# A two-layer encoder on one core: 17 of 44 pairs of W_up's row tiles with seven block products for eight

## The chip, the cores and the metric

The kernel runs on one core of a Trainium2 chip. The metric is device time in microseconds (us) of one execution; lower is better. The inputs lie in device memory when the time begins.

## What is computed

Two layers over 512 positions of 1024 channels, all in float32. The part around the change is the feed-forward block; the rest of a layer is a Fourier group and a windowed attention with 8 heads, joined by W_o.

```python
def reference(x, ...):                      # x: (1, 512, 1024)
    for l in range(2):
        p = rmsnorm(x, norm1[l]) @ w_in[l]
        u, q, k, v = split(p)               # 512 Fourier columns, 8 heads, 2 key and value heads
        y_f = fourier_mix(u, w_fourier[l], b_fourier[l])     # Re(FFT2(u)) @ w_f + b_f
        y_a = windowed_gqa(rope(rmsnorm(q)), rope(rmsnorm(k)), v, sink[l])
        x = x + concat(rmsnorm(y_f), rmsnorm(y_a)) @ w_o[l]
        h = rmsnorm(x, norm2[l])
        up = dwconv_centred(h @ w_up[l], conv_w[l], conv_b[l])   # 3 taps over positions
        gate, val = split(up)               # 2816 columns each
        x = x + (silu(gate) * val) @ w_down[l]
    return x
```

## The kernel before

**Data.** x stays in SBUF, transposed: eight tiles x[k] of 128 channels x 512 positions. A matrix product is made of matmuls with a 128x128 block of weights and up to 512 columns of data. To keep float32's precision, both operands are split into a high and a low part, and mm3 (L114) issues three matmuls into one PSUM bank: high x high (L120), low x high (L121), high x low (L122). Weights are split on the way: wload (L127) loads 512 KB into one of three wraw buffers on SP's queue, wsplit (L132) lets ACT copy the high part of a 512-column chunk into one of five whi buffers and DVE subtract it, for one of five wlo buffers (L140, recorded at L93 with every other tensor_tensor; ACT's instructions are all at L90).

**Names.** A tile's name is its buffer's tag with a number: tF and tA are general temporaries of 512 columns (six each), sq the temporary of squares (two), m4, slab, act and pT larger ones; rb is a row of reciprocal norms copied from PSUM, and nr, computed on POOL at L211, what it is made from. PSUM has eight banks: mm (three), sc (two), tp (two), av (one); the feed-forward block uses six of them in turn (FFN_BANKS). Numbers in the quoted rows tell tiles of one tag apart.

**Order.** The kernel is written for a tile framework: the program gives the operations, and a scheduler with a model of the engines decides in which order each engine's instructions stand; buffers and banks are handed out in the order of the program, and a tile waits until its buffer's last one is done with. issue_after holds an instruction back behind another. Every engine then runs its own list strictly in that order.

**Attention and W_o.** attention(p) (written from L513) treats two heads: for each block of 128 queries PE makes scores (L529), DVE masks them, ACT takes exponentials with their sum, POOL divides (L538), PE transposes (L541), ACT copies the result out of PSUM as pT, PE multiplies with the values (L548). The order in the program is attention(3), attention(0), the Fourier group's output (L634 to L661, tile yf), attention(1), attention(2), W_o. Its first half (L683) needs the Fourier group alone (ys), so that its 96 matmuls can be spread among the steps of attention(1) and (2); mm3's after= and the list steps do that. Its second half (L690) needs the attention. It updates x, and norm_tile makes h2, the split, scaled input of the feed-forward block, with the sum of squares for rb2, the row of reciprocal norms that is multiplied in behind W_up.

**Feed-forward block** (L705 to L761). The 22 tiles of gate columns and the 22 of value columns are paired: pair fi is made of tiles fi and fi + 22. Each tile takes 8 blocks x 3 matmuls of 512 columns, then DVE multiplies by rb2 out of PSUM, ACT and DVE make the three-tap convolution (an activation and two scalar_tensor_tensor at L96), ACT applies silu, the two tiles are multiplied (DVE in layer 0, POOL in layer 1) and split into gu. After 11 pairs W_down's eight tiles take these as input (HALVES). presplit splits layer 1's W_qkv, W_in, W_fourier and W_o during layer 0 and stores the two parts in DRAM, from where layer 1 fetches them; it goes one step ahead at a time, with next(ahead).

## Time and profile before

| | |
|---|---|
| time, median of 3 runs | 1057.46 us (1056.27 to 1057.54) |
| the profiled execution | 1056.14 us, span 1054.3 us |
| granted TensorE clock | 0.999 |
| matmuls | 5107, busy 1038.2 us |
| HBM read, written | 116.02 MB, 23.07 MB |
| W_up | 88 loads of 512.0 KB |

The profile is of one execution. Its engines are PE (matmuls), PEld (loading of weights into PE, beside PE's work), DVE (vector), ACT (scalar), POOL and SP (here a DMA queue). A busy time is the sum over an engine's instructions; what bounds a stage is seen in the stage's own rows, and in what ended the idle time before an instruction ("<-").

### The profile page before, as it was taken

What the parts mean: (1) busy time and instruction counts of PE and PEld (TensorE: products, weight loads), DVE (VectorE), ACT (ScalarE), POOL (GpSimd) and SP (SyncE); (2) the same over time, 40 slices, a digit from 0 to 9 for tenths busy, and PEclk for the clock granted to TensorE, in tenths of its full rate; (3) what the DMA queues carried; (4) which work ended last, traced back from release to release, by engine and by line L of the source; (5) the groups of instructions that cost most, each with busy time, mean ns of one, the idle gap of its engine ahead of it and who ended that gap; (6) DMA issues with size and microseconds to landing.
All of it is one profiled execution on the core that took longest, in us unless ns stands there. A gap on an engine that the chain in (4) does not pass through costs nothing.

```text
span 1054.3 us, 14425 instructions
## 1 busy us (share of the span) xinstructions
PE 1038.2 (98%) x5107; PEld 873.2 (83%) x5107; DVE 726.8 (69%) x1384; ACT 507.9 (48%) x939; POOL 90.8 (9%) x164
## 2 busy tenths in 40 slices
PE   8998999999999999999999999999999999999998
PEld 8986778888888888888899887888888888888887
DVE  8878768697767777777519775478877336878632
ACT  5339755455444445455423785246554224454421
POOL 0004410000000000000000152001101000101100
PEclk9999999999999999999999999999999999999999
DMA  7232152332269833239856313333332333332241
GB/s 273 83 115 87 58 193 81 100 100 96 78 226 353 324 100 101 89 114 322 280 181 221 113 62 99 122 100 94 101 101 74 96 115 100 98 101 82 82 150 48
DMA packets 60475, 140.03 MB, mean 133 GB/s; under 512 B 6642, under 2 KB 22258, under 8 KB 60404
## 3 DMA queue, kind: packets, MB, share of 16 engines
q1 hardware_dynamic: 60404, 139.12, 40.5%
q8 instruction: 40, 0.66, 0.3%
q14 instruction: 31, 0.25, 0.1%
HBM read 116.02 MB, written 23.07 MB: 132 GB/s over the span
## 4 chain that ended last, share of the span: by engine, by line
PE 93%; DVE 2%; DMA 2%; ACT 1%; issue 1%; POOL 0%; SPq 0%; ACTq 0%; DVEq 0%; POOLq 0%
PE ps L122 28%; PE ps L120 28%; PE ps L121 28%; PE ps L118 3%; PE ps L548 2%; PE ps L541 2%; PE ps L529 1%; DMA wraw<-in_w_qkv_dram 1%; PE ps L234 1%; PE ps L227 1%; ACT tA L90 0%; DMA x<-in_xT_dram 0%; DVE tA L533 0%; ACT act L90 0%; PE ps L500 0%
## 5 line engine op out<-in xcount | busy, mean ns | idle before, releaser
L90 ACT ACTIVATE whi<-wraw 128x512 fp32r<-128x512 f32 (+1 forms) x296 | 182.0, 616 | 290.8 <-PE ps L122 278.4
L120 PE MATMUL ps<-act,whi 128*128 128x512 f32 x768 | 298.9, 390 | 0.0
L121 PE MATMUL ps<-act,wlo 128*128 128x512 f32 x768 | 298.3, 389 | 0.0
L122 PE MATMUL ps<-act,whi 128*128 128x512 f32 x768 | 298.2, 389 | 0.0
L93 DVE TENSOR_TENSOR wlo<-wraw,whi 128x512 fp32r<-128x512 f32 (+1 forms) x304 | 219.7, 726 | 103.4 <-ACT whi L90 102.0
L122 PEld LDWEIGHTS ps<-act,whi 128*128 128x128 f32 x768 | 144.2, 188 | 30.1
L120 PEld LDWEIGHTS ps<-act,whi 128*128 128x128 f32 x768 | 144.2, 188 | 29.7
L121 PEld LDWEIGHTS ps<-act,wlo 128*128 128x128 f32 x768 | 144.2, 188 | 29.7
L96 DVE SCALAR_TENSOR_TENSOR tF<-tF,pb,tF 128x511 f32<-128x511 f32 x176 | 133.5, 763 | 11.1 <-ACT tF L90 8.7
L93 DVE TENSOR_TENSOR tF<-ps,rb 128x512 f32<-128x512 f32 x104 | 71.2, 689 | 77.9 <-PE ps L122 64.7
L120 PE MATMUL ps<-slab,whi 128*128 128x512 f32 (+2 forms) x212 | 82.2, 388 | 0.0
L122 PE MATMUL ps<-slab,whi 128*128 128x512 f32 (+2 forms) x212 | 79.9, 380 | 0.4 <-DVE slab L93 0.3
L121 PE MATMUL ps<-slab,wlo 128*128 128x512 f32 (+2 forms) x212 | 80.0, 378 | 0.0
L90 ACT ACTIVATE tF<-tF,pb 128x512 f32<-128x512 f32 x88 | 71.7, 816 | 11.3 <-DVE tF L93 4.6
L93 DVE TENSOR_TENSOR x<-x,ps 128x512 f32<-128x512 f32 (+1 forms) x49 | 32.9, 674 | 36.5 <-PE ps L122 36.3
L93 POOL TENSOR_TENSOR tF<-tF,tF 128x512 f32<-128x512 f32 x22 | 30.2, 1371 | 256.1 <-DVE tF L96 224.1
L120 PE MATMUL ps<-pT,whi 128*128 128x512 f32 (+1 forms) x132 | 50.5, 383 | 0.0
L121 PE MATMUL ps<-pT,wlo 128*128 128x512 f32 (+1 forms) x132 | 50.5, 383 | 0.0
L122 PE MATMUL ps<-pT,whi 128*128 128x512 f32 (+1 forms) x132 | 50.5, 383 | 0.0
L538 POOL TENSOR_SCALAR tA<-tA,den 128x256 f32<-128x256 f32 (+1 forms) x64 | 37.4, 590 | 145.1 <-DVE den L537 144.6
L533 DVE CUSTOM_DVE_ANT_0 tA<-ps,pb,nsink 128x256 f32<-128x256 f32 (+1 forms) x64 | 37.8, 603 | 14.5 <-PE ps L529 9.7
L122 PEld LDWEIGHTS ps<-slab,whi 128*128 128x128 f32 x212 | 39.7, 188 | 8.3 <-DVE slab L93 0.9
(178 smaller groups left out, 1485.0 us busy)
## 6 DMA issues: line engine op xcount, KB each, us to landing
wraw<-in_w_up_dram SPq DMA_DIRECT2D x88, 512.0 KB, 3.5
wraw<-in_w_down_dram SPq DMA_DIRECT2D x32, 512.0 KB, 3.7
kept<-tA SPq DMA_DIRECT2D x56, 256.0 KB, 5.7
whi<-kept SPq DMA_DIRECT2D x28, 256.0 KB, 3.0
wlo<-kept SPq DMA_DIRECT2D x28, 256.0 KB, 3.0
kept<-tA SPq DMA_DIRECT2D x32, 192.0 KB, 4.4
wraw<-in_w_down_dram SPq DMA_DIRECT2D x32, 192.0 KB, 2.4
wraw<-in_w_o_dram SPq DMA_DIRECT2D x8, 512.0 KB, 3.7
```

The lines of the kernel that those rows point to most:

```text
L90: return nc.scalar.activation(out, in_, func, **kw)
L93: return (eng or nc.vector).tensor_tensor(out, a, b, op=op)
L96: return nc.vector.scalar_tensor_tensor(out=out, in0=a, scalar=s, in1=b, op0=op0, op1=op1)
L118: nc.tensor.matmul(out, a[0], b[0], start=start, stop=stop, **kw)
L120: nc.tensor.matmul(out, a[0], b[0], start=start, stop=False, **kw)
L121: nc.tensor.matmul(out, a[1], b[0], start=False, stop=False, **kw)
L122: nc.tensor.matmul(out, a[0], b[1], start=False, stop=stop, **kw)
L227: nc.tensor.matmul(pt[:, 2 * b:2 * b + 2], acc[:, b * P:(b + 1) * P], ones2, start=True, stop=True)
L533: nc.vector.tensor_tensor_reduce(out=pr[:, :n], in0=sc[:, :n], in1=mask[:, m0:m0 + n], scale=qs_scale[p][:, i, e:e + 1], scalar=nsink[:, l ...
L538: nc.gpsimd.tensor_scalar(pr[:, :n], pr[:, :n], den[:, i:i + 1], 1.0, op0=ALU.mult, op1=ALU.mult)
L541: tr = nc.tensor.transpose(pp[:, j * P:(j + 1) * P], pr[:, j * P:(j + 1) * P], ident)
L548: pv = nc.tensor.matmul(py[64 * e:64 * e + 64, i0 * P:(i1 + 1) * P], vp[:, j, 64 * g:64 * g + 64], pT[:, half, e, b0:b0 + 2 * (i1 - i0) + ...
```

## The change

A pair's two tiles and the eight tiles of h make a product of 2 x 2 blocks: the weights' blocks are a11, a12 (tile fi, first and last four k), a21, a22 (tile fi + 22), and h's are first and last four k, positions 0 to 255 and 256 to 511. Block by block this takes eight block products. In 17 of the 44 pairs (layer 0: fi = 2, 5, 8, 11, 14, 17, 20; layer 1: fi = 3, 5, ..., 21) up_seven now takes seven, of sums and differences of blocks, each of 4 k x 3 matmuls of 256 columns. DVE makes the weights' sums (s1 to s4) and all seven low parts; the products are accumulated in PSUM and, between the banks, by ACT's copies and DVE's additions. The sums of h's blocks are made once for a layer (sums_of_h), in the buffers m4, room and others that are free by then.

The other pairs go through up_eight. For one tile of the pair in layer 0 and for both in layer 1 it makes the low part another way (wsplit_add): ACT writes the negated high part to wlo, and a DMA on POOL's queue reads the same weights from DRAM a second time and accumulates them on it (256 KB each, 78 in all).

Besides: three groups of 8, 7 and 7 pairs for two of 11; silu's product on DVE in both layers; the square's temporary from sq to tF everywhere, in attention too; presplit with one matrix part at a time, in a buffer praw of its own, and its ACT copy held behind the pair's last ACT step (pace).

```diff
-HALVES = [(0, 11), (11, 11)]
+GROUPS = [(0, 8), (8, 7), (15, 7)]
+SEVEN = [range(2, FT, 3), range(3, FT, 2)]
...
-             "tA": (512, 6), "tF": (512, 6), "sq": (512, 2)}
+             "tA": (512, 6), "tF": (512, 6), "praw": (512, 2)}
...
+    def wsplit_add(raw, src):
+
+        hi, lo = [wp.tile([P, 512], F32R, tag=z, name=nm(z), bufs=5) for z in ("whi", "wlo")]
+        act(hi, raw)
+        act(lo, f(hi), scale=-1.0)
+        nc.gpsimd.dma_start(lo, src, accum_op=ALU.add)
+        return hi, lo
...
-    def add_square(acc, src, first, tag="sq"):
+    def add_square(acc, src, first, tag="tF"):
...
+    def sums_of_h(l, h2):
+
+        room = rooms()
+        out = []
+        for k in range(4):
+            b = [temp(512, "tF") for _ in range(2)]
+            for i in range(2):
+                act(b[i], x[k + 4 * i], scale=g2[:, l, k + 4 * i:k + 4 * i + 1])
+            t13, t24 = temp(512, "tF"), temp(512, "tF")
+            tt(t13[:, LO], b[0][:, HI], b[0][:, LO], ALU.subtract)
+            tt(t13[:, HI], b[1][:, HI], b[0][:, HI], ALU.subtract)
+            tt(t24[:, LO], t13[:, LO], b[1][:, HI], ALU.subtract)
+            tt(t24[:, HI], t24[:, LO], b[1][:, LO], ALU.add)
+            r13, r24 = [next(room), next(room)], [next(room), next(room)]
+            split(*r13, t13)
+            split(*r24, t24)
...
+    def up_eight(l, fi, h2, ts, rb2):
+        for z in range(2):
+            m = fi + z * FT
+            raw = wload(t["w_up"][l, m], 1024)
+            w = [wsplit_add(raw[:, c:c + 512], t["w_up"][l, m, :, c:c + 512]) if l or z else wsplit(raw[:, c:c + 512])
+                 for c in (0, 512)]
...
+    def up_seven(l, fi, h2, ts, rb2):
+        a, b = [wload(t["w_up"][l, fi + z * FT], 1024) for z in range(2)]
+        a11, a12, a21, a22 = a[:, :512], a[:, 512:], b[:, :512], b[:, 512:]
+        xy, zz = bank(), bank()
+        X, Y, Z = xy[:, LO], xy[:, HI], zz[:, LO]
+        ua, ub = temp(512, "tF"), temp(512, "tF")
+
+        def product(o, w, key, start=False):
+            for k in range(4):
+                mm3(o, [z[:, k * P:(k + 1) * P] for z in w], ts[k][key], start and k == 0, k == 3, skip_group_check=True)
+
+        product(X, wsplit(a11), "B11", True)
+        act(ua[:, LO], X)
+        s1, s2, s3, s4 = [temp(512, "tA") for _ in range(4)]
+        tt(s1, a21, a22, ALU.add)
+        product(Y, wsplit(s1), "T1")
+        act(ub[:, HI], Y)
+        tt(s3, a11, a21, ALU.subtract)
+        tt(s2, s3, a22, ALU.subtract)
+        product(X, wsplit(s2), "T2")
+        act(ua[:, HI], X)
+        product(Z, wsplit(a12), "B21", True)
+        tt(ua[:, LO], ua[:, LO], Z, ALU.add)
+        product(X, wsplit(s3), "T3")
+        tt(ub[:, HI], ub[:, HI], X, ALU.add)
+        tt(s4, a12, s2, ALU.add)
+        product(Y, wsplit(s4), "B22")
+        tt(ua[:, HI], ua[:, HI], Y, ALU.add)
+        tt(ua, ua, rb2, ALU.mult)
+        yield ua
+        product(X, wsplit(a22), "T4")
+        tt(ub[:, LO], X, rb2[:, LO], ALU.mult)
+        tt(ub[:, HI], ub[:, HI], rb2[:, HI], ALU.mult)
+        yield ub
...
-        for f0, nf in HALVES:
+        ts = sums_of_h(l, h2)
+        for f0, nf in GROUPS:
...
+                ys_ = [conv(l, fi + z * FT, u) for z, u in enumerate((up_seven if fi in SEVEN[l] else up_eight)(l, fi, h2, ts, rb2))]
+                next(ahead)
                 act(ys_[0], ys_[0], AF.Silu)
-                tt(ys_[0], ys_[0], ys_[1], ALU.mult, nc.gpsimd if l else nc.vector)
+                tt(ys_[0], ys_[0], ys_[1], ALU.mult)
```

The scheduler gives other lists for it. A row below is an instruction: line, operation, output <- inputs, shape; "x2" is two in a row. (Line numbers of the changed kernel differ: its matmuls of mm3 are at L121 to L123, attention's at L634, L646 and L653, tensor_tensor at L94, the accumulating DMA at L141.)

PE, layer 0, attention(1) and (2), before: tiles ps_334, ps_335 and ps_341 are the first outputs of W_o's first half, between transposes and scores.

```order
L541 MATMUL ps_279_1273<-ident_113,tA_278_1267 128x128 x3
L541 MATMUL ps_282_1287<-ident_113,tA_281_1281 128x128 x3
L120 MATMUL ps_334_1506<-slab_261_1217,whi_330_1498 128x512
L121 MATMUL ps_334_1506<-slab_261_1217,wlo_331_1499 128x512
L120 MATMUL ps_335_1520<-slab_261_1217,whi_332_1502 128x512
L121 MATMUL ps_335_1520<-slab_261_1217,wlo_333_1503 128x512
L541 MATMUL ps_285_1307<-ident_113,tA_284_1301 128x128 x3
L120 MATMUL ps_341_1544<-slab_261_1217,whi_337_1536 128x512
L121 MATMUL ps_341_1544<-slab_261_1217,wlo_338_1537 128x512
L529 MATMUL ps_292_1339<-m4_99_562,act_153_801 128x256 x2
L529 MATMUL ps_303_1370<-m4_100_563,act_156_814 128x256 x2
L122 MATMUL ps_334_1506<-slab_261_1217,whi_330_1498 128x512
```

PE now, where the first of the same W_o matmuls stand: the rows ahead are the last transposes and value products of attention(2).

```order
L646 MATMUL ps_323_1467<-ident_113,tA_322_1461 128x128 x2
L653 MATMUL ps_297_1364<-pT_302_1369,v_26_180 64x256 x4
L653 MATMUL ps_297_1364<-pT_302_1369,v_26_180 64x128 x2
L646 MATMUL ps_326_1480<-ident_113,tA_325_1474 128x128 x2
L241 MATMUL ps_259_1209<-ident_113,nr_258_1206 128x128 x4
L653 MATMUL ps_297_1364<-pT_302_1369,v_26_180 64x128 x2
L653 MATMUL ps_297_1364<-pT_302_1369,v_26_180 64x256 x4
L121 MATMUL ps_334_1506<-slab_261_1217,whi_330_1498 128x512
L122 MATMUL ps_334_1506<-slab_261_1217,wlo_331_1499 128x512
L121 MATMUL ps_335_1520<-slab_261_1217,whi_332_1502 128x512
L122 MATMUL ps_335_1520<-slab_261_1217,wlo_333_1503 128x512
L121 MATMUL ps_341_1544<-slab_261_1217,whi_337_1536 128x512
```

All 96 matmuls of W_o's first half have moved behind attention(2).

POOL, layer 0, end of attention to the rstd of the feed-forward block (nr_416), before:

```order
L532 COPY tA_325_1474<-nsink_122 128x1
L538 TENSOR_SCALAR tA_316_1433<-tA_316_1433,den_299_1366 128x384
L538 TENSOR_SCALAR tA_319_1447<-tA_319_1447,den_301_1368 128x384
L538 TENSOR_SCALAR tA_322_1461<-tA_322_1461,den_299_1366 128x256
L538 TENSOR_SCALAR tA_325_1474<-tA_325_1474,den_301_1368 128x256
L211 TENSOR_TENSOR nr_359_1654<-nv_358_1653,mhalf_120 128x4
L211 TENSOR_TENSOR nr_416_1885<-nv_415_1884,mhalf_120 128x4
```

POOL now, the same place; the accumulating transfers of pair 0's second tile and of the first chunk of pair 1's have come ahead of nr_416.

```order
L637 COPY tA_322_1461<-nsink_122 128x1
L637 COPY tA_325_1474<-nsink_122 128x1
L643 TENSOR_SCALAR tA_322_1461<-tA_322_1461,den_299_1366 128x256
L643 TENSOR_SCALAR tA_325_1474<-tA_325_1474,den_301_1368 128x256
L218 TENSOR_TENSOR nr_258_1206<-nv_257_1205,mhalf_120 128x4
L218 TENSOR_TENSOR nr_359_1654<-nv_358_1653,mhalf_120 128x4
L141 DMA wlo_467_2034<-in_w_up_dram 128x512
L141 DMA wlo_469_2039<-in_w_up_dram 128x512
L141 DMA wlo_490_2133<-in_w_up_dram 128x512
L218 TENSOR_TENSOR nr_416_1885<-nv_415_1884,mhalf_120 128x4
L141 DMA wlo_492_2138<-in_w_up_dram 128x512
```

nr_416 now stands behind three transfers, the third of which needs wlo_490.

DVE, layer 0, from the first instructions that use rb_418 (the row rb2), before:

```order
L93 TENSOR_TENSOR tF_437_1959<-ps_436_1934,rb_418_1893 128x512
L93 TENSOR_TENSOR wlo_496_2210<-wraw_492_2203,whi_495_2209 128x512
L93 TENSOR_TENSOR tF_445_2000<-ps_444_1975,rb_418_1893 128x512
L96 SCALAR_TENSOR_TENSOR tF_438_1961<-tF_437_1959,pb_96,tF_438_1961 128x511
L93 TENSOR_TENSOR tF_454_2046<-ps_453_2021,rb_418_1893 128x512
L96 SCALAR_TENSOR_TENSOR tF_438_1961<-tF_437_1959,pb_96,tF_438_1961 128x511
L96 SCALAR_TENSOR_TENSOR tF_446_2002<-tF_445_2000,pb_96,tF_446_2002 128x511
L93 TENSOR_TENSOR wlo_502_2247<-wraw_500_2244,whi_501_2246 128x512
L93 TENSOR_TENSOR tF_467_2095<-ps_466_2070,rb_418_1893 128x512
L96 SCALAR_TENSOR_TENSOR tF_455_2048<-tF_454_2046,pb_96,tF_455_2048 128x511
```

DVE now, the last 12 rows up to wlo_515, the low part of the first seven pair's second weights; eight rows ahead of them stands the first that uses rb_418, and ahead of that the sums of h.

```order
L97 SCALAR_TENSOR_TENSOR tF_472_2070<-tF_471_2068,pb_96,tF_472_2070 128x511
L94 TENSOR_TENSOR tF_494_2167<-ps_493_2142,rb_418_1893 128x512
L97 SCALAR_TENSOR_TENSOR tF_487_2126<-tF_486_2124,pb_96,tF_487_2126 128x511
L94 TENSOR_TENSOR tF_464_2027<-tF_464_2027,tF_472_2070 128x512
L97 SCALAR_TENSOR_TENSOR tF_495_2169<-tF_494_2167,pb_96,tF_495_2169 128x511
L94 TENSOR_TENSOR tA_498_2176<-praw_474_2076,tA_497_2175 128x384
L94 TENSOR_TENSOR tA_510_2213<-wraw_503_2190 128x512
L94 TENSOR_TENSOR tA_512_2215<-wraw_502_2188,wraw_503_2190 128x512
L97 SCALAR_TENSOR_TENSOR tF_495_2169<-tF_494_2167,pb_96,tF_495_2169 128x511
L94 TENSOR_TENSOR slab_479_2086<-tF_464_2027,slab_479_2086 128x512
L94 TENSOR_TENSOR tA_511_2214<-tA_512_2215,wraw_503_2190 128x512
L94 TENSOR_TENSOR wlo_515_2219<-tA_510_2213,whi_514_2218 128x512
```

Between rb_418 and wlo_515 the convolutions of two pairs, two low parts of the next layer's weights and three sums of weight blocks have come in.

More of the change, by code (lines that the diff above doesn't have):

```diff
@@ L136, in wsplit @@
         if hi_eng is None:
-            act(hi[:, :n], raw)
+            pace[0] = act(hi[:, :n], raw).ins
         else:
@@ L155, in keep @@
             two = [temp(n, "tA", F32R) for _ in range(2)]
-            split(two[0], two[1], src)
+            with tc.issue_after(pace[0]):
+                act(two[0], src)
+            tt(two[1], src, f(two[0]), ALU.subtract)
             kept[key] = [dp.tile([P, n], F32, tag=f"{key}{s}", name=nm("kept")) for s in range(2)]
@@ L741, in encoder_kernel @@
                 next(ahead)
-                next(ahead)
-                w = []
-                for c in range(0, nf, 8):
-                    n = min(8, nf - c)
-                    w += wchunks(t["w_down"][l, m, :, (f0 + c) * P:(f0 + c + n) * P], n * P)
+                w = wchunks(t["w_down"][l, m, :, f0 * P:(f0 + nf) * P], nf * P)
                 end = l == L - 1 and f0 + nf == FT
```

103 lines of the change are left out of this document (53 added, 50 removed).

## The prediction

> **What bounds the kernel now.** I read the page first: busy times, then the engines of the chain of work that ended last.
>
> ```profile
> PE 1038.2 (98%) x5107; PEld 873.2 (83%) x5107; DVE 726.8 (69%) x1384; ACT 507.9 (48%) x939; POOL 90.8 (9%) x164
> ...
> PE 93%; DVE 2%; DMA 2%; ACT 1%; issue 1%; POOL 0%; SPq 0%; ACTq 0%; DVEq 0%; POOLq 0%
> ```
>
> PE is busy for 1038.2 of 1054.3 us and carries 93% of the chain: only 16 us of its idle time are left, so a gain must come from less matmul time. Next the busy times by stage: W_up of layer 0 and of layer 1 (columns: window, length, then PE, PEld, DVE, ACT, POOL, clock, DMA share, GB/s).
>
> ```profile
> 200.00:250.00 50.00, 50.00 (x222) 41.40 (x221) 45.00 (x70) 30.27 (x46) 0.00 (x0) 1.00 0.30 95
> 850.00:900.00 50.00, 50.00 (x223) 41.38 (x222) 27.13 (x38) 18.32 (x28) 2.58 (x2) 1.00 0.32 101
> ```
>
> PE has no gap there. A matmul of 512 columns takes 50/222 = 0.2252 us. DVE is already at 45.0 of 50 in layer 0; its durations overlap a little, as the rows further down show.
>
> **The change part by part: matmuls.** For 256 columns the timeline has the halved last product of layer 1, 60 matmuls from the first row here to the last.
>
> ```profile
> 1043.70 0.28 PE L120 MATMUL ps<-slab,whi 128*128 128x256 f32 x1
> ...
> 1050.78 0.28 PE L122 MATMUL ps<-m,whi 128*128 128x256 f32 x1
> ```
>
> 7.08/59 = 0.120 us each, more than half of 0.2252. A pair of eight products is 48 x 0.2252 = 10.81 us, one of seven 7 x 4 x 3 = 84 x 0.120 = 10.08: 0.73 saved, and over 17 pairs **12.4 us**. That is all there is to gain; everything below is a loss against it. [...]
>
> **DVE and ACT in the FFN.** Durations of W_up in layer 0 by form, then two rows of the timeline that show that starts lie closer than durations.
>
> ```profile
> L93 DVE TENSOR_TENSOR wlo<-wraw,whi 128x512 fp32r<-128x512 f32 x40 | 27.6, 690 | 3.3 <-ACT whi L90 3.1
> L96 DVE SCALAR_TENSOR_TENSOR tF<-tF,pb,tF 128x511 f32<-128x511 f32 x37 | 27.6, 750 | 2.3 <-ACT tF L90 1.9
> L93 DVE TENSOR_TENSOR tA<-m,tA 128x384 fp32r<-128x384 f32 x8 | 4.4, 556 | 6.3 <-ACT tA L90 6.2
> ...
> L93 DVE TENSOR_TENSOR tA<-m 128x255 f32<-128x255 f32 x8 | 3.0, 419 | 0.0
> ...
> 170.31 0.68 DVE L93 TENSOR_TENSOR acc<-acc,sq 128x512 f32<-128x512 f32 x1
> 170.91 0.68 DVE L93 TENSOR_TENSOR x<-x,tF 128x512 f32<-128x512 f32 x1
> ```
>
> 0.68 long, 0.60 apart: DVE is really taken for 0.08 less than a duration, so 0.61 for a full tensor_tensor, 0.67 for a step of the convolution, 0.34 for a half-width one. A seven pair needs 4 sums of weight blocks, 7 low parts, the product with the rstd row, silu's product and the split of the result (14 x 0.61), 4 convolution steps (2.7) and 5 half-width accumulations (1.7): **12.9 us, against 10.08 on PE**. An eight pair needs 6.3 in layer 0 (two of its four low parts come by transfers), 5.1 in layer 1 (all do), against 10.81. The sums of h at each start are 16 half-width ones and 8 splits, 10.3. Layer 1: 10 x 12.9 + 12 x 5.1 + 10.3 = 201, against 10 x 10.08 + 12 x 10.81 = 231 on PE. So DVE bounds neither layer, but every seven pair leaves it 2.8 us behind, and PE's lead over a weight is at most the five wlo buffers, 5 x 12 x 0.120 = 7.2 us. Hidden where DVE enters with that lead, 2.8 where it doesn't: 0 to 15 x 2.8 = 42 over the pairs behind the first one of each layer; the spare 4.5 to 5.7 of the eight pair between puts it near the low end. I take **+3**.
>
> **Silu's product** goes from POOL back to DVE in layer 1 (0.61 x 22, in the 5.1 and 12.9 above). What that returns:
>
> ```profile
> L93 POOL TENSOR_TENSOR tF<-tF,tF 128x512 f32<-128x512 f32 x22 | 30.2, 1371 | 256.1 <-DVE tF L96 224.1
> ...
> L93 DVE TENSOR_TENSOR wlo<-wraw,whi 128x512 fp32r<-128x512 f32 x35 | 32.5, 930 | 2.7 <-ACT whi L90 2.3
> ```
>
> In 900 to 1000 us the low parts took 930 ns in the mean, beside 690 in layer 0: some waited out a POOL product. Both are under a busy PE: 0 now and 0 after.
>
> **Accumulating transfers.** 78 of 256 KB (30 in layer 0, 48 in layer 1), issued on POOL's queue behind ACT's negated high part. No transfer of before accumulates; the nearest rows are these, read from and stored to DRAM at the same size (last column: us to landing).
>
> ```profile
> kept<-tA SPq DMA_DIRECT2D x56, 256.0 KB, 5.7
> whi<-kept SPq DMA_DIRECT2D x28, 256.0 KB, 3.0
> ```
>
> 3.0 to 5.7 us, with ACT's 0.6 ahead, against a lead of five chunks of 12 x 0.2252 = 2.7, that is 13.5: hidden unless the buffer is released late. 0 to 14: the upper end has one in five late by a third of a chunk's time, 16 x 0.9. I take **+1**, nearer to the 3.0 of the row that also writes wlo. [...]
>
> **Attention loses its filling.** The square's temporary moves from its own buffers to tF, in attention too, so the Fourier part's output products, which need tF as well, come behind the end of attention(0), and all 96 matmuls of W_o's first half behind the last attention step (front, PE's order); before, they stood between the attention's matmuls. ACT then sets the pace. ACT's rows, for layer 0 and for layer 1 (first window of each: its start):
>
> ```profile
> 87.90:112.10 24.20, 23.19 (x158) 18.85 (x160) 19.59 (x68) 22.76 (x64) 12.01 (x32) 1.00 0.22 73
> 87.90:139.40 51.50, 49.76 (x318) 39.06 (x319) 41.43 (x126) 43.32 (x118) 22.20 (x53) 1.00 0.24 79
> ...
> 606.10:632.00 25.90, 24.54 (x195) 20.72 (x195) 19.80 (x69) 22.46 (x66) 14.79 (x35) 1.00 0.19 63
> 606.10:662.00 55.90, 54.21 (x367) 43.54 (x368) 36.12 (x115) 37.08 (x106) 22.75 (x53) 1.00 0.26 86
> ...
> L90 ACT ACTIVATE whi<-wraw 128x512 fp32r<-128x512 f32 x7 | 4.4, 628 | 3.5 <-PE ps L122 3.2 <-PE ps L118 0.3
> L90 ACT ACTIVATE slab<-tF 128x512 fp32r<-128x512 f32 x4 | 2.4, 642 | 0.0
> L90 ACT ACTIVATE tA<-m 128x384 fp32r<-128x384 f32 x4 | 2.1, 522 | 0.4 <-DMA kept<-tA 0.4
> L90 ACT ACTIVATE rb<-ps 128x512 f32<-128x512 f32 x1 | 0.6, 574 | 0.0
> ...
> 149.58 0.39 PE L120 MATMUL ps<-act,whi 128*128 128x512 f32 x1
> ...
> 665.92 0.39 PE L120 MATMUL ps<-act,whi 128*128 128x512 f32 x1
> ```
>
> ACT's 43.32 us from 87.9 on, without the slab splits (2.4), the rstd row (0.6), four of seven weight splits (2.5) and the next layer's weights (2.1), all of which stand behind attention's end afterwards, are 35.7. At the 94% that ACT reached in the first 24.2 us (22.76) they last 38.0, to 125.9; at 80% 44.6, to 132.5. Row copy, scaling, split and low part take some 3.5 (0.6 + 0.75 + 0.64 + 0.69 from the rows and PE's transposes), and 96 x 0.2252 = 21.6 follow with nothing beside them: W_o's second half begins at 151.0 to 157.6, not at 149.58. +1.4 to +8; I take **+4**. Layer 1: 37.08 - 2.5 - 0.6 = 34.0; at 94% to 642.3, at the 87% measured there (22.46/25.90) to 645.2; with 3.5 and 21.6 W_o's second half begins at 667.4 to 670.3, not 665.92: +1.5 to +4.4, **+2.5**.
>
> **The first seven pair of layer 0** is the third pair. Count from T, where W_o's second half begins. PE comes to its second product after 96 + 96 matmuls of full width and 12 of half, T + 44.7, or some T + 46.4 with the transposes and a short wait for wlo_490 or wlo_492 (the buffer of wlo_490 is free at T + 32.4, when the first pair is through; 0.6 on ACT and the 3.0 to 5.7 bring it to T + 36 to 39, and PE asks for it at T + 38.0). This product needs wlo_515. DVE makes it as the 20th instruction from the first that needs rb_418 (front, DVE's order): 10 x 0.61 + 8 x 0.67 + 2 of 384 columns at 0.48 = 12.4. rb_418 needs nr_416, which stands on POOL behind three accumulating transfers, whose third waits for that same wlo_490; PE's transposes of it stand 78 matmuls behind W_o, T + 39.2, and ACT has it at some T + 41. So wlo_515 is there at T + 53.4: a stall of 7. Were rb_418 free at T + 37, 3; were it as late as in before (T + 49.7), 15:
>
> ```profile
> 199.28 0.60 ACT L90 ACTIVATE rb<-ps 128x512 f32<-128x512 f32 x1 [2.52 <-PE ps L234]
> ```
>
> In before nothing waits for it at that time, as six PSUM banks take two more tiles. I take **+7**. Layer 1 begins its sevens one pair later, with six banks to run through, but its rstd stands behind six transfers: **+1**, 0 to 8.
>
> **Hidden, at nothing:** three groups for two (the W_down products are the same matmuls, and PE has other pairs' work ahead at a border; 1 to 2 us each if not), and the next layer's weights one at a time (transfers of under 6 us with a pair, 10.8 us, between).
>
> **The sum:** -12.4 + 3 + 1 + 4 + 2.5 + 7 + 1 = +6.1. On the profiled execution, 1056.14, that is 1062.2; the median of the runs is 1.3 above it, so **1063.5 us**.
>
> **Rivals.**
> - *Faster:* ACT keeps 94% in both layers (1.4 + 1.5), rb_418 is early (3), and the bursts of DVE hide (0 to 1): -12.4 + 7 = -5.4, 1052; with the start hidden too, 1049. For it: PE's lead of up to 7.2 us covers 2.8, and the eight pairs lie between. Against: the rstd's place behind three transfers. 0.30.
> - *DVE sets the seven pairs:* with half of their 42 us shown, +18 more, 1081. It decides where DVE enters a pair without a lead, that is with an eight pair's convolutions still queued ahead. For it: 45.0 of 50 busy in layer 0 already. 0.12.
> - *Late transfers:* landing at over twice 5.7, 13.5 us, a transfer uses up the lead of five chunks, and the 14 of the upper bound are shown in place of 1: 1076. 0.10.
> - *The price goes with the columns:* 84 x 0.1126 = 9.46 would save 1.35 a pair, 23 in all, and give 1053. Against it stand the 60 matmuls at 0.120. [...] 0.03.
> - *My forecast,* with losses between the bounds of the terms, 1055 to 1072: 0.45.
>
> **How the numbers follow.** A measurement of this kernel can tell about 0.2%, 2.1 us, from no change: 1055.3 to 1059.6 counts as the same. Faster: 0.30 + 0.03 and 0.01 of my own case; same: 0.08, the low end of my own case; the rest slower, 0.58. The range goes from 1047 (the faster rival with every stall gone) to 1081 (the DVE rival at half); outside lie the worst of DVE and transfers.
>
> **What would show it.** In the profile after: 256-column matmuls 0.120 us apart; W_o's first half in one run of 96 behind attention, its second beginning at 151 to 157 and some 2.5 later than 665.9 less what was gained; PE idle behind the first product of the first seven pair, released by DVE's wlo; wlo transfers landing in 3 to 6 us. If PE waits at seven pairs all along, the DVE rival holds; if at weights of eight pairs with a DMA as releaser, the transfers'. My forecast is wrong if W_o's second half begins at 149.6 or earlier, or if no stall stands in the third pair.

## The result, and the profile after

| | before | after |
|---|---|---|
| time, median | 1057.38 us | 1162.93 us (1159.3 to 1165.58, 4 runs) |
| ratio | | 1.0998, 95% interval 1.0967 to 1.1029 |
| span of the profiled execution | 1054.3 us | 1160.9 us |
| granted TensorE clock | 0.999 | 0.975 |

The change makes the kernel 10% slower. The forecast was 1063.5 in a range of 1047 to 1081: the sign was right, the size was off by a factor of 17. The page after: busy times, the chain by engine, and the longest of PE's waits (sum, times, longest).

```profile
PE 1067.0 (92%) x5707; PEld 910.6 (78%) x5707; DVE 785.1 (68%) x1579; ACT 601.8 (52%) x1151; POOL 125.9 (11%) x220
...
PE 72%; DVE 9%; DMA 9%; ACT 5%; issue 5%; POOL 0%; SPq 0%; DVEq 0%; POOLq 0%; ACTq 0%
...
PE ps L121 <- ACT whi L91: 21.4, 6, 5.1
PE ps L122 <- DMA wlo<-in_w_up_dram: 20.2, 12, 4.0
PE ps L121 <- ACT tF L91: 17.9, 29, 1.5
PE ps L122 <- DVE wlo L94: 11.9, 11, 1.8
```

PE's idle time went from 16 to 94 us. It waits mainly for four things, none of which is in the rows of before: a high part from ACT, an accumulating transfer, an ACT copy out of PSUM (tF), a low part from DVE. DVE's share of the span is no higher than before (68% for 69%) and ACT's little higher (52% for 48%); neither has become a bound by its load.

Two stretches of W_up, to set beside those of before, and one wait with what followed it (the third number from the end of a row is the granted clock):

```profile
200.00:250.00 50.00, 38.85 (x200) 33.11 (x199) 39.31 (x66) 30.02 (x52) 3.43 (x4) 0.91 0.53 144
900.00:950.00 50.00, 41.78 (x239) 36.02 (x237) 30.47 (x50) 26.28 (x46) 5.18 (x6) 0.97 0.43 105
...
203.30:206.70 3.40, 0.00 (x0) 0.00 (x0) 3.40 (x7) 3.32 (x7) 0.00 (x0) 1.00 0.32 120
206.70:213.50 6.80, 3.95 (x16) 3.66 (x17) 6.80 (x12) 3.95 (x8) 0.00 (x0) 0.50 0.22 61
```

For 3.4 us PE does nothing, and in the 6.8 us that follow its clock is granted at 0.50. The trace has eleven such stretches at half clock, 58 us in all, each beginning in or shortly behind a wait and 3.4, 6.8 or 10.2 us long; before had none but in its last microsecond. Only one of the eleven has 3.4 us without any matmul in front of it (the last section has more on this).

In these stretches matmuls of 256 columns start 0.213 us apart in place of 0.120, those of 512 columns 0.427 in place of 0.227. By the 145 and 31 of them that start there, half clock takes some 20 us of the 106; the rest of the 58 us is time in which PE waits as well.

Where the 106.6 us lie, by parts of the span (W_o(1) is W_o's second half; a part runs from the first matmul of one to the first of the next; idle time and stretches at half clock are PE's):

| part | before | after | idle before, after | half clock after |
|---|---|---|---|---|
| start to W_o(1) of layer 0 | 149.58 | 155.53 | 8.9, 12.1 | 0 |
| to W_qkv of layer 1 (layer 0's W_up and W_down) | 384.55 | 438.42 | 0, 37.8 | 44.4 |
| to W_o(1) of layer 1 | 131.79 | 138.82 | 4.0, 6.4 | 3.4 |
| to the end (layer 1's W_up and W_down) | 388.43 | 428.16 | 0, 34.5 | 10.2 |

Layer 0's part: 37.8 idle + 14.6 for the half clock - 5.1 saved (7 x 0.73) = 47.3, measured 53.9. Layer 1's: 34.5 + 4.8 - 7.3 = 32.0, measured 39.7. Most of the rest, 6.6 and 7.7, is waiting that does not show as idle time: the modelled end of a matmul lies some 0.16 us behind the next one's start, so each of the 23 and 37 waits costs that much more (3.7 and 5.9), and shorter ones show nothing.

Three chains make the waits. **A bank shared.** In layer 1, PE's last matmul of a seven pair's first product, its next product, and ACT meanwhile:

```profile
845.29 0.28 PE L123 MATMUL ps<-act,whi 128*128 128x256 f32 x1
847.08 0.39 PE L121 MATMUL ps<-m,whi 128*128 128x256 f32 x1 [1.51 <-ACT tF L91]
847.31 0.28 PE L122 MATMUL ps<-m,wlo 128*128 128x256 f32 x1
...
848.49 0.28 PE L123 MATMUL ps<-room,whi 128*128 128x256 f32 x1
849.25 0.39 PE L121 MATMUL ps<-m,whi 128*128 128x256 f32 x1 [0.47 <-ACT tF L91]
...
845.61 0.63 ACT L91 ACTIVATE whi<-wraw 128x512 fp32r<-128x512 f32 x1
846.15 0.61 ACT L91 ACTIVATE tF<-tF 128x512 f32<-128x512 f32 x1
846.67 0.36 ACT L91 ACTIVATE tF<-ps 128x256 f32<-128x256 f32 x1
```

The product at 847.08 goes to Y, which is the other half of the bank that holds X. Nothing of Y's values depends on X, but PE waits until ACT has copied X (846.67 to 847.03), and ACT has a high part and a silu ahead of that copy. The waits of 0.47 and 0.24 come back at all ten seven pairs of layer 1, the one of 1.5 at six of them.

**A place on DVE's list.** In layer 0, ahead of the second seven pair, DVE:

```profile
242.72 0.69 DVE L94 TENSOR_TENSOR tF<-ps,rb 128x512 f32<-128x512 f32 x1
...
244.29 0.75 DVE L97 SCALAR_TENSOR_TENSOR tF<-tF,pb,tF 128x511 f32<-128x511 f32 x1 [0.29 <-ACT tF L91]
244.96 0.55 DVE L94 TENSOR_TENSOR tA<-praw,tA 128x384 fp32r<-128x384 f32 x1
245.43 0.68 DVE L94 TENSOR_TENSOR tA<-wraw 128x512 f32<-128x512 f32 x1
246.03 0.69 DVE L94 TENSOR_TENSOR tA<-wraw,wraw 128x512 f32<-128x512 f32 x1
```

s1, which needs nothing but weights (245.43), stands behind the row at 242.72, which can begin only when PE has finished the pair before. From there PE waits for s1's high part and low part (2.84 and 1.42 us), whatever lead the buffers would allow.

**Transfers behind a seven pair.** In layer 1: the negated high part on ACT, the transfer's issue on POOL, its landing (start and length in the chain), PE's wait:

```profile
915.51 0.63 ACT L91 ACTIVATE wlo<-whi 128x512 fp32r<-128x512 f32 x1
...
916.43 0.86 POOL L141 DMA_DIRECT2D wlo<-in_w_up_dram  x1 [17.31 <-ACT wlo L91]
...
916.43 6.35 DMA wlo<-in_w_up_dram
...
922.83 0.50 PE L122 MATMUL ps<-act,wlo 128*128 128x512 f32 x1 [3.98 <-DMA wlo<-in_w_up_dram]
...
wlo<-in_w_up_dram POOLq DMA_DIRECT2D x78, 256.0 KB, 5.1
```

From the start on ACT to the landing it is 7.3 us. The buffers ahead of this one hold the seven pair's last weights, and PE is through with each of them in 1.44 us.

### The profile page after: what moved, and what is told of

The parts are those of the page before. It is cut to its first block, busy times and chain, and to the rows that moved or that the text cites. A ratio compares the mean times of both kernels' runs of the same rounds, so it can differ in the third digit from the quotient of the medians.

```text
span 1160.9 us, 16272 instructions
## 1 busy us (share of the span) xinstructions
PE 1067.0 (92%) x5707; PEld 910.6 (78%) x5707; DVE 785.1 (68%) x1579; ACT 601.8 (52%) x1151; POOL 125.9 (11%) x220
## 3 DMA queue, kind: packets, MB, share of 16 engines
q1 hardware_dynamic: 60468, 139.12, 37.8%
## 4 chain that ended last, share of the span: by engine, by line
PE 72%; DVE 9%; DMA 9%; ACT 5%; issue 5%; POOL 0%; SPq 0%; DVEq 0%; POOLq 0%; ACTq 0%
PE ps L122 22%; PE ps L121 21%; PE ps L123 21%; DMA wlo<-in_w_up_dram 7%; PE ps L119 3%; DVE tF L97 2%; DVE tA L94 2%; ACT tF L91 1%; ACT tA L91 1%; PE ps L653 1%; DVE wlo L94 1%; DVE tF L94 1%; DVE tA L638 1%; PE ps L634 1%; PE ps L646 1%
## 5 line engine op out<-in xcount | busy, mean ns | idle before, releaser
L122 PE MATMUL ps<-act,wlo 128*128 128x512 f32 (+1 forms) x700 | 257.8, 369 | 22.1 <-DMA wlo<-in_w_up_dram 20.2
L123 PE MATMUL ps<-act,whi 128*128 128x512 f32 (+1 forms) x700 | 254.5, 365 | 0.0
L121 PE MATMUL ps<-act,whi 128*128 128x512 f32 (+1 forms) x700 | 252.2, 366 | 0.5 <-DVE tF L94 0.5
L94 DVE TENSOR_TENSOR wlo<-wraw,whi 128x512 fp32r<-128x512 f32 (+1 forms) x209 | 134.8, 655 | 65.2 <-ACT whi L91 64.5
L121 PEld LDWEIGHTS ps<-act,whi 128*128 128x128 f32 x700 | 135.9, 194 | 21.0 <-DVE tF L94 0.7
L123 PEld LDWEIGHTS ps<-act,whi 128*128 128x128 f32 x700 | 135.4, 194 | 19.4
L141 POOL DMA_DIRECT2D wlo<-in_w_up_dram x78 | 67.7, 868 | 702.4 <-ACT wlo L91 343.7
L121 PE MATMUL ps<-slab,whi 128*128 128x512 f32 (+2 forms) x276 | 105.3, 384 | 2.9 <-ACT slab L91 2.6
L123 PE MATMUL ps<-slab,whi 128*128 128x512 f32 (+2 forms) x276 | 104.6, 381 | 1.0 <-DVE slab L94 1.0
L94 DVE TENSOR_TENSOR tF<-ps,rb 128x512 f32<-128x512 f32 (+1 forms) x87 | 53.7, 633 | 55.5 <-PE ps L123 53.9
L121 PE MATMUL ps<-m,whi 128*128 128x256 f32 x170 | 54.6, 321 | 39.2 <-ACT whi L91 21.4
L94 DVE TENSOR_TENSOR x<-x,ps 128x512 f32<-128x512 f32 (+1 forms) x65 | 42.8, 675 | 53.5 <-PE ps L123 53.5
L121 PEld LDWEIGHTS ps<-m,whi 128*128 128x128 f32 x170 | 35.1, 207 | 48.6 <-ACT tF L91 24.9
L91 ACT ACTIVATE whi<-tA 128x512 fp32r<-128x512 f32 x68 | 42.5, 627 | 56.9 <-PE ps L123 41.9
L121 PEld LDWEIGHTS ps<-slab,whi 128*128 128x128 f32 x276 | 51.9, 188 | 14.3 <-ACT slab L91 3.5
L121 PE MATMUL ps<-pT,whi 128*128 128x512 f32 (+1 forms) x163 | 62.6, 386 | 0.0
```

Of the source, the lines that this page charges most:

```text
L91: return nc.scalar.activation(out, in_, func, **kw)
L94: return (eng or nc.vector).tensor_tensor(out, a, b, op=op)
L121: nc.tensor.matmul(out, a[0], b[0], start=start, stop=False, **kw)
L122: nc.tensor.matmul(out, a[1], b[0], start=False, stop=False, **kw)
L123: nc.tensor.matmul(out, a[0], b[1], start=False, stop=stop, **kw)
L141: nc.gpsimd.dma_start(lo, src, accum_op=ALU.add)
```

## The experiments

Theory A: the seven pairs' waits come from these three chains, one by one, with the half clock behind them. Rival B: the accumulating transfers are too slow in themselves. Rival C: DVE (or ACT) has too much work. For attention, theory D (the square in tF) stands against rival E (the rest of the change). Where parts are given, they are the four of the table above in its order, from the profiled execution. A run without a ratio is a single execution; the changed kernel's four lie between 1159.3 and 1165.6, so a few us between single runs say little, and the parts and waits say more. In twelve of the eighteen traces PE has a stretch at half clock that begins 26.0 to 28.4 us after the start, ahead of all that the change touches (in the run with the square apart the mean clock from 26.0 to 29.9 us is 0.73); it is worth 0.6 to 2.1 us of the first part.

**No seven pair** (left out: the seven-product form; the sums of h are made for nothing).

```diff
-SEVEN = [range(2, FT, 3), range(3, FT, 2)]
+SEVEN = [(), ()]
```

> All 44 pairs in eight products; the sums of h are still made, but nothing uses them; the accumulating transfers grow from 78 to 132. Theory A (the stalls come from the seven pairs: they use up PE's lead, and the transfers right behind one have only its 5 x 1.44 = 7.2 us of lead): layer 0 from W_o's second half to W_qkv of layer 1 within 3 us of the 384.6 before, layer 1 from W_o's second half to the end within 4 of 388.4, clock 1.0, in all 1066 to 1072 with what attention lost. Rival B (the transfers are too slow in themselves, 1.8 us to issue and 4 to 8 to land): more of them, so idle time at eight pairs stays or grows, 1090 or more.

1067.23 us; parts 159.10, 382.79, 137.11, 386.46.

```profile
PE 1042.8 (98%) x5095; PEld 875.2 (82%) x5095; DVE 668.5 (63%) x1338; ACT 594.9 (56%) x1103; POOL 173.1 (16%) x274
```

No idle time in either feed-forward part, with 132 transfers in place of 78. They land 5.2 us after their issue in the median and 7.9 at the most (5.1 and 8.0 in the changed kernel), so they are as slow here and not late: as the cause of the feed-forward parts' loss B falls. The attention parts are 9.5 and 5.3 longer than before, the feed-forward parts 1.8 and 2.0 shorter, as 16 small matmuls for attention's row of reciprocal norms (some 1.6 us) have moved from each of these into the part ahead. Together that is the 11 us that are left of the slow-down.

**No transfers.** Eight pairs' low parts all on DVE.

```diff
-            w = [wsplit_add(raw[:, c:c + 512], ...) if l or z else wsplit(raw[:, c:c + 512])
+            w = [wsplit(raw[:, c:c + 512])
```

> Eight pairs make all their low parts on DVE, no accumulating transfer; the seven pairs stay. Theory A: the 20 us of waits for transfers go, with the half clock that follows some of them, the waits of the seven pairs stay: 1130 to 1140, layer 1's part 428 -> 410 to 415. Rival C (DVE has too much work, the transfers relieve it): 2.4 us more on DVE for each eight pair of layer 1 and 1.2 in layer 0, so no faster than 1160, perhaps slower.

1178.78 us; parts 158.27, 434.72, 140.57, 443.44. A's forecast of 1130 to 1140 was wrong, C's (no faster than 1160) held. PE's waits:

```profile
PE ps L121 <- ACT tF L91: 47.0, 19, 5.5
PE ps L121 <- ACT whi L91: 25.8, 7, 6.7
PE ps L122 <- DVE wlo L94: 13.4, 11, 2.0
```

The waits for transfers are gone, and in layer 1 one of some 5 us for the copy of X has come to most of the seven pairs (eight of ten, 4.4 to 5.5). More work on DVE makes the convolutions of the pair before later, ACT's silu waits for them, and the copy stands behind it. DVE is busy 303.6 of these 443 us: it is not out of capacity, it is late on a list with no slack. So C is right that DVE's work matters, and the transfers do relieve it; not by its sum.

**Y apart.** Y goes into Z's bank.

```diff
-        X, Y, Z = xy[:, LO], xy[:, HI], zz[:, LO]
+        X, Y, Z = xy[:, LO], zz[:, LO], zz[:, HI]
...
-        product(Y, wsplit(s1), "T1")
+        product(Y, wsplit(s1), "T1", True)
...
-        product(Z, wsplit(a12), "B21", True)
+        product(Z, wsplit(a12), "B21")
```

> The product Y goes into the bank of Z instead of that of X, everything else as it is. Theory A (in layer 1 PE waits at each seven pair for ACT to copy X out of the bank that Y's product writes next: 17.9 us in 29 waits): most of these waits go, layer 1's part 428 -> 412 to 418, total 1145 to 1152, layer 0 about as it was. Rival C (ACT's or DVE's load): the waits move to another product, total unchanged within 5.

1125.81 us; parts 156.57, 420.70, 137.09, 409.68.

```profile
PE ps L121 <- ACT whi L91: 19.2, 6, 5.1
PE ps L122 <- DMA wlo<-in_w_up_dram: 16.5, 9, 3.0
PE ps L122 <- DVE wlo L94: 8.9, 6, 1.8
PE ps L121 <- ACT tF L91: 5.0, 5, 3.1
```

The waits for the copy fall from 17.9 to 5.0, and layer 1's part by 18.5 (A had 412 to 418 for it). Layer 0 gains as much, 17.7, which I had not expected: 9.6 of idle time and 13.7 us of half clock less. Its waits for transfers, five in the changed kernel, are gone, and none of the waits left for one lies in layer 0; why they were late only with the shared bank was not followed further.

**Layer 1 only.**

```diff
-SEVEN = [range(2, FT, 3), range(3, FT, 2)]
+SEVEN = [(), range(3, FT, 2)]
```

> Layer 0 with 22 eight pairs (44 transfers), layer 1 as it is. Theory A: layer 0's part from 438.4 back to 385 to 390 and no half clock in it, total 1108 to 1115. Rival B (slow transfers): waits for transfers remain in layer 0, 400 or more there, total over 1125.

1115.93 us; parts 158.72, 383.22, 138.69, 433.52. Layer 0 is whole again, with its transfers; its loss belongs to its seven pairs alone. Against B once more. Layer 1's part, with nothing changed in it, came out 5.4 longer than in the changed kernel, with 10.2 us more at half clock; why was not followed.

**The square apart.**

```diff
-            add_square(accA, py, first_pair)
+            add_square(accA, py, first_pair, tag="praw")
```

> The changed kernel with one edit: the temporary of attention's square goes to the buffer praw, which is free during attention, and no longer to tF. Theory D (attention lost its filling because the square takes a tF buffer ahead of the Fourier group's output): W_o's second half begins at 149 to 151 in place of 155.5, and from W_qkv of layer 1 to W_o's second half it takes 132 to 134 in place of 138.8; in all about 1151. Rival E (the rest of the change sets attention's pace, ACT's extra work for instance): both within 2 us of the changed kernel's.

1159.91 us; parts 151.11, 442.71, 131.55, 432.78. W_o's second half begins as follows, in layer 0 and in layer 1:

```profile
151.11 0.39 PE L121 MATMUL ps<-act,whi 128*128 128x512 f32 x1
...
725.37 0.39 PE L121 MATMUL ps<-act,whi 128*128 128x512 f32 x1
```

W_o's first half begins at 116.0 us again, among the attention's matmuls (114.5 before, 131.1 in the changed kernel), and both attention parts return to what they were, within 1.6 us, by this one buffer. D holds, E falls. The total gains 3 and not 11: the feed-forward parts came out 4 and 5 us longer in this execution, with other waits.

**Sums early**, with Y apart: the loads, the first high part and s1 to s3 are written into the program ahead of the product with rb2 of the pair before.

```diff
+            if z and fi + 1 in SEVEN[l]:
+                heads[l, fi + 1] = head(l, fi + 1)
             u = temp(512, "tF")
             tt(u, o, rb2, ALU.mult)
             yield u
...
+    def head(l, fi):
+        a, b = [wload(t["w_up"][l, fi + z * FT], 1024) for z in range(2)]
+        a11, a12, a21, a22 = a[:, :512], a[:, 512:], b[:, :512], b[:, 512:]
+        s1, s2, s3, s4 = s = [temp(512, "tA") for _ in range(4)]
+        w11 = wsplit(a11)
+        tt(s1, a21, a22, ALU.add)
+        tt(s3, a11, a21, ALU.subtract)
+        tt(s2, s3, a22, ALU.subtract)
+        return a, b, s, w11, wsplit(s1)
```

> As the run with Y apart, and the loads, the first high part and the sums s1 to s3 of a seven pair are written ahead of the product with the rstd row of the pair before, so that on DVE they no longer stand behind its last convolution. Theory A (in layer 0 it is this place on DVE's list that makes PE wait, 19.2 us for whi and 8.9 for wlo with Y apart, and the half clock after it): these waits go for the most part, layer 0's part 420.7 -> 390 to 400, total 1098 to 1108. Rival C (DVE has too much to do in those pairs, whatever the order): the waits come back at later products, layer 0 still over 412, total over 1118.

1115.58 us; parts 158.34, 406.05, 137.09, 412.19.

```profile
PE ps L122 <- DMA wlo<-in_w_up_dram: 20.9, 12, 3.4
PE ps L121 <- ACT tF L91: 7.8, 9, 3.1
PE ps L121 <- ACT whi L91: 6.3, 6, 2.0
PE ps L122 <- DVE wlo L94: 5.1, 6, 2.7
```

The waits for whi and wlo fall from 28.1 to 11.4, layer 0's part by 14.7, to between A's 390 to 400 and C's 412: the place on the list was a cause, as A has it, though the edit brings forward the loads and the first split too. Of layer 0's 17.5 us of idle time 4.5 stand at its first seven pair, 5.1 are waits for transfers, and the rest is spread over the other pairs. PE's waits for transfers grow by 4.4 in all.

**Split behind**, with Y apart.

```diff
-... if l or z else wsplit(
+... if z or (l and fi - 1 not in SEVEN[l]) else wsplit(
```

> As the run with Y apart, but in layer 1 the tile right behind a seven pair gets its low parts from DVE and not by a transfer (20 transfers fewer). Theory A (only these transfers are late, since PE's lead there is made of products of 1.44 us): layer 1's waits for transfers go, its part 409.7 -> 393 to 399, total 1109 to 1115; layer 0 as it was. Rival C (DVE's load, as the run without any transfer showed): the waits move to the seven pairs, layer 1's part 405 or more.

1105.84 us; parts 155.74, 420.65, 137.09, 390.55. PE no longer waits for a transfer at all, and layer 1's part falls by 19.1, below A's 393 to 399 and to within 2.1 of before. A holds: in layer 1 late were only the transfers right behind a seven pair (and those of the chunks after).

**All four edits.**

> All four edits together: Y apart, sums early, the tile behind a seven pair split on DVE, the square in praw. Theory A and D: attention as before the change, each layer's part at 384 to 394 with clock 1.0 for the most part, in all 1050 to 1072. Rival C: DVE's load keeps over 15 us of waits at the seven pairs in each layer, over 1085.

1092.19 us; parts 150.91, 407.01, 131.55, 400.95. A, which ended at 1072, is missed. The time is C's (over 1085); of its 15 us of waits at the seven pairs of each layer there are some 13 and 11 (17.5 and 13.4 of idle time, with 4.1 and 1.7 for transfers in them). Layer 1 is 10.4 longer than without the early sums. The later runs are for this rest.

**Every fourth pair in layer 1**, else the changed kernel.

```diff
-SEVEN = [range(2, FT, 3), range(3, FT, 2)]
+SEVEN = [range(2, FT, 3), range(3, FT, 4)]
```

> The changed kernel with 5 seven pairs in layer 1 in place of 10 (every fourth pair). Theory A (each seven pair and the tile behind it cost their own waits): layer 1 loses half of what it lost, 386.5 + 5 x 4.9 - 5 x 0.73 = about 407 for its part in place of 428.2, total about 1140. Rival C (too much work on DVE): with 12.9 - 5.1 = 7.8 us less on DVE for each pair turned back, 39 us in all, its load is far below PE's and the waits vanish: layer 1's part under 392, total under 1127.

1143.09 us; layer 1's part 410.92, near A's 407 and far from C's 392: half the seven pairs lose 24.5 of the 41.7 us (both against the 386.46 without any), although DVE then has 39 us less to do. In the kernel as changed each costs its own, 4 to 5 us, whatever the load.

**No seven pair, and the square apart.**

> No seven pair, the square in praw: what is left of the change are three groups, the accumulating transfers (132), silu's product on DVE and the next layer's weights one at a time. Theory A and D: nothing waits any more, attention as before, 1054 to 1058. Rival B (the transfers cost something in themselves): over 1060.

1061.03 us, ratio 1.003 (1.0016 to 1.0045). That is above the 1054 to 1058 of A and D and at B's mark of over 1060. The remainder of the change by itself brings nothing and costs some 3 us; 2.6 of them are in layer 1's part, with 2.3 us of waits for transfers in its first and third pair; layer 0 has one more, 0.6, in its fifth. So much of B is right: in this run some early transfers of a layer are late with no seven pair near.

**All four edits, five seven pairs in layer 1** (5, 9, 13, 17, 21).

```diff
-SEVEN = [range(2, FT, 3), range(3, FT, 2)]
+SEVEN = [(), range(5, FT, 4)]
```

> All four edits, seven products only in five pairs of layer 1 (5, 9, 13, 17, 21). Theory A: each saves 0.73 and costs some 1 us in waits for ACT's copy and the restart of PE, so 1055 to 1061, no better than the kernel without any. If the waits are hidden at this spacing, 1051 to 1054, better than both kernels.

1055.63 us, ratio 0.999 (0.9978 to 1.0001); parts 149.85, 385.40, 131.51, 386.99. Spaced like this PE waits at no seven pair, and layer 1's part is 4.0 shorter than in the run without any (390.98); 5 x 0.73 = 3.65 would be their saving. That only makes up for what else the change costs: against before the interval still holds 1.

**Layer 0 later**, all four edits.

```diff
-SEVEN = [range(2, FT, 3), range(3, FT, 2)]
+SEVEN = [range(5, FT, 3), range(3, FT, 2)]
```

> The run of all four edits with layer 0's first seven pair at 5 instead of 2 (6 sevens there). Theory F (the first seven pair waits for the rstd row whatever else is mended: 8.8 us of waits at 204 to 211 us and 10.2 us of half clock): layer 0's part 407.0 -> 391 to 396, layer 1's as it was at 401, total about 1078. Rival C (load): layer 0's part stays above 400, the waits come later.

1080.99 us; parts 151.27, 396.77, 131.65, 399.46. Moving the first seven pair takes 10.2 us off layer 0's part, to 0.8 above F's range and below C's 400: at place 2 it waits whatever the buffers do (4.2 and 2.5 us with all four edits), as F has it.

**Every fourth pair in both layers**, all four edits, the first two pairs of layer 1 without transfers.

> All four edits, every fourth pair from 5 on in both layers (5 + 5), and the first two pairs of layer 1 without transfers. Theory A (a seven pair costs nothing where an eight pair or three stand between and its sums come early): layer 0's part 385.4 -> 382 to 384, layer 1's 387.0 -> 385 to 386, in all 1050 to 1054, better than before. Rival C (the next layer's weights and the two low parts that eight pairs of layer 0 leave to DVE make sevens there cost more): layer 0's part over 388, total over 1057.

1058.01 us, ratio 1.0019 (1.0004 to 1.0033); parts 153.19, 388.65, 131.59, 387.26. In layer 0 three waits for transfers, 4.5 us, and the 3.4 us at half clock behind one take more than the seven products save. Part and total are C's (over 388, over 1057), the waits are the transfers'.

**Every third pair in layer 1**, likewise.

> All four edits, layer 0 without sevens, layer 1 with every third pair from 5 on (6), its first two pairs without transfers. Theory A: 387.0 -> 384 to 386 for layer 1's part, total 1053 to 1055. Rival C (closer spacing brings the waits back, as every second pair did with 401): 388 or more, total over 1056.5.

1063.22 us, ratio 1.0061 (1.0041 to 1.0082); layer 1's part 393.90. With two eight pairs between sevens waits are back, 6.0 us: 2.5 in W_down, the longest of them for weights whose load landed late, 2.0 for the layer's first transfers, 1.6 at two of the six seven pairs. The time is C's.

**No early sums, every second pair of layer 1**: Y apart, split behind, the square apart, layer 0 without sevens.

> Y apart, split behind, the square apart, no early sums; layer 0 without sevens, layer 1 with every second pair (10). If the early sums made the rest in layer 1 (theory G): its part 389 to 391, as in the run without them, total 1055 to 1058. If it was the spacing (rival C): 398 or more, total over 1064.

1064.09 us, ratio 1.0063 (1.0051 to 1.0076); layer 1's part 395.75, between G and C: not decided. Its first seven pair waits 3.1 us for ACT's copy, with 6.8 us of half clock, seven others 0.8 each.

**No early sums, every fourth pair of layer 1**, its first two pairs without transfers.

> The same with every fourth pair of layer 1 from 5 on (5), and its first two pairs without transfers. Theory G: a seven pair still waits 0.9 us for ACT's copy and saves 0.73, so nothing is gained by fewer or more: layer 1's part 385 to 388, total 1052 to 1055, better than before by the waits that fall away at its start. Rival C: as the run with early sums at this spacing, 387, total 1055 to 1056.

1056.95 us, ratio 0.9993 (0.9984 to 1.0002); layer 1's part 387.44. There is no wait at a seven pair, where G had 0.9. At this spacing the early sums make no difference (386.99 with them); at every second pair they cost up to 5 (401 against 395.8). How that rest divides between sums and spacing stays open. No version came out clearly faster than the kernel before.

## Why the prediction failed, point by point

- **Saving, -12.4: right.** The 256-column matmuls of the seven pairs stand 0.118 to 0.120 us apart (848.49 - 847.31 over 10 steps), and five of them without waits gave 4.0 where 3.65 was worked out.
- **First seven pair of layer 0, +7: right in time and in DVE's list, wrong on POOL.** ACT, DVE, PE and POOL, with T = 155.53:

```profile
197.13 0.60 ACT L91 ACTIVATE rb<-ps 128x512 f32<-128x512 f32 x1 [1.64 <-PE ps L241]
...
209.40 0.68 DVE L94 TENSOR_TENSOR wlo<-tA,whi 128x512 fp32r<-128x512 f32 x1
...
202.28 0.39 PE L123 MATMUL ps<-act,whi 128*128 128x512 f32 x1
207.72 0.58 PE L121 MATMUL ps<-m,whi 128*128 128x256 f32 x1 [5.06 <-ACT whi L91]
210.13 0.58 PE L122 MATMUL ps<-m,wlo 128*128 128x256 f32 x1 [1.82 <-DVE wlo L94]
...
190.51 1.14 POOL L218 TENSOR_TENSOR nr<-nv,mhalf 128x4 f32<-128x4 f32 x1 [1.58 <-DVE nv L216]
```

  rb_418 at T + 41.6 (forecast T + 41), wlo_515 ready at T + 54.6 (53.4), PE there at T + 47.1 (46.4), idle 5.06 + 1.82 = 6.9 (7). The longer wait is for ACT's high part of s1 and not for DVE's wlo; that part waits for s1 on the same DVE list. nr_416 was ready at T + 36, with POOL idle 1.58 us ahead of it for DVE: the three transfers in front of it, on which the forecast leant, held nothing up, and the time of rb_418 was that of PE's transposes behind their 78 matmuls. The half clock behind the stall was not in the sum.
- **Attention, +4 and +2.5: right in cause, low in layer 1 (its bound was +4.4).** Measured +5.95 and +7.0. The rows behind attention: W_o's first half, and its second in layer 0 and layer 1.

```profile
131.06 0.50 PE L121 MATMUL ps<-slab,whi 128*128 128x512 f32 x1 [1.31 <-ACT slab L91]
...
155.53 0.48 PE L121 MATMUL ps<-act,whi 128*128 128x512 f32 x1
...
732.77 0.48 PE L121 MATMUL ps<-act,whi 128*128 128x512 f32 x1
```

  W_o's first half begins at 131.1, within the 129.4 to 136.0 that ACT's pace gave. From there to the second half it takes 24.5 us in both layers, where 21.6 were counted: the 16 small matmuls of the second half's rstd row, left out of the forecast, stand there now. In before they stood behind the beginning of the second half, so some 1.6 us of each measured figure have only moved from the next part.
- **The seven pairs' own waits, +3: the step that failed.** The forecast held that DVE's 2.8 us a pair are hidden "where DVE enters with that lead", and counted load and buffers. It never followed one pair through PE, ACT and DVE. Two of the three chains can be read without a run: the copies of X and Y between products are in the diff, with X and Y in one bank, and s1's place behind the convolution of the pair before is in DVE's new order, of which I had used only the first pair's rows. The waits measured on PE are 21.4 + 17.9 + 11.9 us, some 7 of them the first pair's; a term of 3 stood for what measured over 40.
- **Layer 1's start, +1, and the terms at nothing: right in size.** PE's only wait for a low part from DVE in layer 1, 1.30 us, stands at its first seven pair; whether the rstd row put it there was not followed. The run without sevens has no idle time at the borders of groups or beside the next layer's weights.
- **Transfers, +1: failed by the lead.** A lead of five chunks of 2.7 us holds between eight pairs (no wait in the run without sevens); behind a seven pair the five buffers ahead are products of 1.44, which the forecast had itself computed two paragraphs earlier. The trace has 20.2 us in 12 waits; a transfer lands 5.1 us after its issue in the median, inside the bounds of 3.0 to 5.7 and above the 3.0 taken, and 8.0 at the most.
- **Half clock: no term at all.** Some 20 us. Before has no wait in W_up, and so no row that shows what a wait does to the clock; the changed kernel's trace is the first here that does (0.50 behind the wait at 203.3).
- **The rivals.** "DVE sets the seven pairs" came nearest in its point of decision (an eight pair's convolutions still queued ahead) and fell short in price, 1081. "Late transfers" was right too. They were priced as alternatives, and they came together, with one unforeseen and the clock on top; the range, built from one at a time, could not hold that.

## What to carry to other kernels

Where PE is busy all the time, a form with less matmul time but more steps between matmuls has to be followed through one unit of work, instruction by instruction on each engine's list: what must PE's next product wait for, and what stands ahead of that on the other lists. Sums of load per engine say only whether it could work. A lead counted in buffers is worth the time of the products that lie in them, so it shrinks exactly where products get shorter (here from 5 x 2.7 to 5 x 1.44 us); and in the changed kernel half clock behind waits of PE cost up to 2.7 us more each time (at the most 29 matmuls of 256 columns, from 490.05 us on, 0.213 us apart in place of 0.120).

## What the runs showed of the hardware that was not expected

- In the trace of the changed kernel each stretch at half clock begins a whole number of times 3.413 us behind the first, to within 0.01 us. Cut at that step, its feed-forward parts have ten pieces at full clock with half clock behind them, and PE was busy in 0 to 45% of each; in the 226 pieces with full clock behind them it was busy in 49% or more. Over all eighteen traces the two ranges overlap, between 45 and 50%. The length of a wait does not part the two kinds here: two pieces ahead of half clock (PE busy 1.55 and 1.54 us, with waits of 1.87 and 1.88 us), one ahead of full clock with a wait of 1.72 us (busy 1.69), and two, both ahead of full clock, between which a wait of 2.31 us is shared (busy 2.33 and 1.94):

```profile
824.55:827.97 3.42, 1.55 (x10) 1.26 (x10) 0.84 (x2) 1.52 (x3) 1.73 (x2) 1.00 0.95 217
947.43:950.85 3.42, 1.54 (x12) 1.34 (x11) 1.54 (x3) 2.34 (x5) 0.86 (x1) 1.00 0.88 214
974.74:978.15 3.41, 1.69 (x13) 1.49 (x13) 1.54 (x3) 2.76 (x5) 1.10 (x3) 1.00 0.80 179
1036.18:1039.59 3.41, 2.33 (x17) 1.80 (x15) 0.70 (x2) 2.31 (x5) 1.73 (x2) 1.00 0.76 181
1039.59:1043.00 3.41, 1.94 (x8) 1.61 (x9) 0.83 (x3) 0.48 (x1) 0.86 (x1) 1.00 1.01 252
```

  In that trace's attention parts, with their small matmuls, half clock followed one piece with PE busy in 75%, and did not follow seven with 61 to 72%. No run moved a wait and nothing else: what of this is the cause was not shown.
- An accumulating transfer of 256 KB took 0.86 us on POOL and landed 3.7 to 8.0 us after its issue, 5.1 in the median, where plain loads of the same size on SP's queue took 3.1 to 3.3.
